# Equal pieces in the mixed expert units, shorter arithmetic of a recurrence, and filter spectra summed in PSUM: a hybrid backbone layer on one Trainium2 core

## Chip, core and metric

The kernel runs on one core of one Trainium2 chip. The metric is device microseconds of one execution, as the median over runs. The core's engines are TensorE (PE, with its weight loads PEld), VectorE (DVE), ScalarE (ACT), GpSimd (POOL) and SyncE (SP), which issues the DMA transfers here.

## What is computed

One layer (depth 1, batch 1) over 512 latent tokens of width 1024, with 256 context tokens ahead of them. All data are f32. Cut to what matters:

```python
p  = modulate(rmsnorm(x),   sh1, sc1)   @ w_in      # sh.., sc.., g.. from silu(c) @ w_ada + b_ada
pc = modulate(rmsnorm(ctx), csh1, csc1) @ w_in
# head group A: width 512, both directions, context first, then latents
u = dwconv(p[:, 512:1024])                          # 4 taps
r, i = sigmoid(block_diag(u, wa, ba)), sigmoid(block_diag(u, wx, bx))
log_a = -8 * r * softplus(-lam)
a, b = exp(log_a), sqrt(-expm1(2 * log_a)) * (i * u)
h[t] = a[t] * h[t-1] + b[t]                         # linear scan
ya = gelu(p[:, :512]) * (h_forward + h_backward)
# head group B: two long convolutions with generated filters
z = v
for o in range(2): z = gates[o] * (irfft(rfft(z, 1024) * rfft(g[o] / sum|g[o]|)) + z * fb[o])
x = x + g1 * (concat(rmsnorm(ya), rmsnorm(z)) @ w_out)
# MoE: best of 4 groups, best 2 of its 8 experts, 32 experts in all
h = modulate(rmsnorm(x), sh2, sc2)
for e: out += combine[:, e] * ((silu(h @ w_gate[e]) * (h @ w_up[e])) @ w_down[e])
return rmsnorm(x + g2 * out) * final_g
```

## The kernel before

Every operation is first recorded and then put in order by a list scheduler (class Recorder): it plays the engines forward with a cost for each operation, repeats this with changed priorities, and the best order found is emitted, with a sequence of its own for each engine. So all recorded work stands at two lines of the profile, L560 (a fixed engine) and L567 (operations written for `X`, where the scheduler may choose DVE, ACT or POOL). A change of one operation can move others.

*Filters* (`filters`, L980). For each of two orders `o`, `ab` holds two combinations (i = 0, 1) of the filter, each with its positions taken apart by residue r modulo 4. `dft` (L1023) multiplies the 128 positions of a residue by a table `dff[:, r, cs]` (cosine or sine) into a PSUM bank. The four outputs of an (o, i) are sums and differences of these transforms, the residues 0 and 2 in one, 1 and 3 in the other. Before the change each residue's product stands in a bank of its own; three of the six are copied to SBUF (`dft_s`), sums go to the tile `PM`, and sums of PM's parts are the outputs.

*Recurrence* (`lru_pair`, L1235, called twice, for two blocks of 128 channels each, the tokens of context and latents in 768 columns). `split` (L1182) takes an f32 operand apart into a rounded part (type fp32r, which PE passes once) and the rest, so that three rounded products stand for one f32 product. Here it was used for the gate weights `lw` and for `v`. The root is written as sqrt(tanh(-log_a) * (a*a + 1)), with DVE's product a*a ahead of the sum.

*Experts.* Each expert has a fixed number of token places (CAPS: sorted by load, the first three 64, then 192, 128, 128, 96, nine of 64, fifteen of 32, one of none). The token places are gathered in 14 units of 128 rows at most; a unit is a list of segments (first column, width, expert, first token) of width 64 or 32. Most units are uniform: two segments of 64 or four of 32. Two are mixed, 64 + 32 + 32: the last of kind M (the odd expert of 64 with two of 32) and the last of kind H (the expert of 96 with one of 32). ORDER, "MMHMQHQAMHQ", says in which order units follow the first three experts, so the mixed ones are the third last and the second last. `expert_units` (L1852) records a unit's work; its inner function `product` (L1870) accumulates gate (8 steps of 128 rows), up (8) and down (two halves of 4): in a step each segment has one matmul, whose token columns are the stationary tile at columns p0 to p0 + w of the array and whose 512 weight columns stream through. The segments' output goes to rows p0 to p0 + w of one PSUM bank.

The weights come in loads of 1 MB (`load`, L1801, issued at L1818), six for each expert, into a ring of 16 slots; a load waits until PE has used what its slot held. The loads stand on SP's queue in the order of use; those behind the first three experts also need the routing's result, since the expert's number is read from it.

The main lines of `product`:

```python
for i, (k, kk, h) in enumerate(parts):
    for (p0, w), wv in zip(sub[0], sub[2]):
        o = T.matmul(b[p0:p0 + w, :nc_], lhs[:, k, p0:p0 + w], wv(m, kk, h)[:, c0:c0 + nc_], start=i == 0,
                     stop=i == len(parts) - 1, tile_position=(0, p0), skip_group_check=True)
```

Of the kernel before, what the change touches and what calls it, by code (L numbers as in the profile page):

```python
# [742 lines left out]
def kernel(ctx: ExitStack, tc: tile.TileContext, a: dict, out: bass.AP, dbg=None):  # L743
# [35 lines left out]
    def give(*vs):  # L779
        for v in vs:  # L780
            v.home.give(v)
# [13 lines left out]
    class Fixed:  # L795
        n = 0
# [106 lines left out]
    SP.dma_start(out=dff[:], in_=a["c_dff"])  # L903

# [75 lines left out]
    def filters(o):  # L980
# [14 lines left out]
        for r in range(4):  # L995
            mab = take("mab", [512])
            mbb = take("mbb", [512])
            S.activation(mab[:], ab[:, 0, r], AF.Abs)
            S.activation(mbb[:], ab[:, 1, r], AF.Abs)
            X.tensor_tensor(mab[:], mab[:], mbb[:], op=OP.max)  # L1000
            give(mbb)
            T.matmul(b[32 * r:32 * r + 32, :], onesf, mab[:], start=True, stop=True,
                     tile_position=(0, 32 * r), skip_group_check=True)
            give(mab)
# [18 lines left out]
        def dft(i, cs, r):  # L1023
            b = ps()
            T.matmul(b, dff[:, r, cs], ab[:, i, r], start=True, stop=True)
            return b

        def dft_s(i, cs, r):
            b = dft(i, cs, r)
            t = take("fa", [512])  # L1030
            X.copy(t[:], b)
            return t

        for i in range(2):
            PM = take("PM", [4, 512])
            t = dft_s(i, i, 2)
            b = dft(i, i, 0)
            V.tensor_tensor(PM[:, 0], b, t[:], op=OP.add)
            V.tensor_tensor(PM[:, 2], b, t[:], op=OP.subtract)
            give(t)  # L1040
            t = dft_s(i, i, 3)
            b = dft(i, i, 1)
            V.tensor_tensor(PM[:, 1], b, t[:], op=OP.add)
            give(t)
            t = dft_s(i, 1 - i, 3)
            b = dft(i, 1 - i, 1)
            V.tensor_tensor(PM[:, 3], b, t[:], op=OP.subtract)
            give(t)
            for g, (p_, op) in enumerate(((0, OP.add), (0, OP.subtract), (2, (OP.add, OP.subtract)[i]),
                                          (2, (OP.subtract, OP.add)[i]))):  # L1050
                t = take("gout", [512])
                X.tensor_tensor(t[:], PM[:, p_], PM[:, p_ + 1], op=op)
                SP.dma_start(out=gd[o, i, g], in_=t[:])
                give(t)
            give(PM)
# [63 lines left out]
    give(*decs, hd, fbias)  # L1119
# [59 lines left out]
    V.tensor_scalar(ncoef, t8[4], 16.0, None, op0=OP.mult)  # L1179


    def split(src, wh, wl):  # L1182

        X.copy(wh, src)
        X.tensor_tensor(wl, src, wh.bitcast(F32), op=OP.subtract)
# [34 lines left out]
    lwH, lwL = (takeR("lw", [16, 128]) for _ in range(2))  # L1220
    split(lw, lwH, lwL)
    give(lw)
# [12 lines left out]
    def lru_pair(blks):  # L1235
        vs, sts = {}, {}
# [20 lines left out]
        for bk, v in vs.items():  # L1257
            st = sts[bk] = takeR("vst", [2048], late=True)
            X.copy(st[:, :768], v)
            X.tensor_tensor(st[:, 768:1536], v, st[:, :768].bitcast(F32), op=OP.subtract)  # L1260
        its = [(bk, d) for bk in blks for d in range(2)]
        rt, it = {}, {}
        for bk, d in its:
            for m, (dst, bn) in enumerate(((rt, "ba"), (it, "bx"))):
                g = take("g", [768])
                gi = (d * 2 + m) * 4 + bk
                b1, b2 = ps(), ps()
                for b, c0, n in ((b1, 0, 256), (b2, 256, 512)):
                    for j, (w, o) in enumerate(((lwH, 0), (lwH, 768), (lwL, 0))):
                        T.matmul(b[:, :n], w[:, gi], sts[bk][:, o + c0:o + c0 + n], start=j == 0, stop=j == 2)  # L1270
                S.activation(g[:, :256], b1[:, :256], AF.Sigmoid, bias=col(bn, 4 * d + bk))
                S.activation(g[:, 256:], b2, AF.Sigmoid, bias=col(bn, 4 * d + bk))
                dst[bk, d] = g
        give(*sts.values())
        at, bt = {}, {}
# [3 lines left out]
        for bk, d in its:  # L1279
            at[bk, d] = take("at", [768])  # L1280
            S.activation(at[bk, d][:], rt[bk, d][:], AF.Exp, scale=coef[:, 4 * d + bk:4 * d + bk + 1])
            S.activation(rt[bk, d][:], rt[bk, d][:], AF.Tanh, scale=ncoef[:, 4 * d + bk:4 * d + bk + 1])
            q = take("q", [768])
            X.tensor_tensor(q[:], at[bk, d][:], at[bk, d][:], op=OP.mult)
            V.scalar_tensor_tensor(rt[bk, d][:], q[:], 1.0, rt[bk, d][:], op0=OP.add, op1=OP.mult)
            give(q)
        for bk, d in its:
            S.activation(rt[bk, d][:], rt[bk, d][:], AF.Sqrt)
            X.tensor_tensor(rt[bk, d][:], rt[bk, d][:], it[bk, d][:], op=OP.mult)
# [188 lines left out]
    while left:  # L1478
        k = left.pop(0)
        i = int(k[1:] or 0)  # L1480
        if k[0] == "L":
            lru_pair((i, i + 1))
            if not [x for x in left if x[0] == "L"]:
                give(lwH, lwL)
# [367 lines left out]
    def expert_units(subs, need=lambda m: None, then=lambda: None, last=False):  # L1852
# [17 lines left out]
        def product(sub, m, lhs, parts, c0=0, nc_=512):  # L1870
            b, before = ps(), None
            for i, (k, kk, h) in enumerate(parts):
                for (p0, w), wv in zip(sub[0], sub[2]):
# [163 lines left out]
```

## Time and profile before

| | us |
|---|---|
| median of 3 runs | 927.65 |
| lowest and highest | 925.95, 929.68 |
| the profiled execution | 931.36 |
| its span in the profile | 929.6 |
| granted TensorE clock, mean | 0.971 of full speed |

How to read it: the span runs from the first to the last instruction of the profiled execution. PE, PEld, DVE, ACT and POOL are busy times of engines, which overlap. In the tables by stage the numbers behind an x count instructions; PEclk is the granted TensorE clock as a part of full speed, DMA the mean busy share of the 16 DMA engines. Names such as bank (a PSUM bank), slot and arena (pieces of SBUF that the kernel hands out) are the program's. An f32 matmul leaves two records in PE's rows, a rounded one (fp32r) one.

### The profile page before, as it was taken

How to read it: one execution, taken by the hardware profiler on the slowest of the kernel's cores; microseconds unless marked ns; L12 is line 12 of the kernel's file. 1: busy time of each engine (PE TensorE's matmuls, PEld its weight loads, DVE VectorE, ACT ScalarE, POOL GpSimd, SP SyncE). 2: the span in 40 equal slices, each digit the busy share in tenths (PEclk: the TensorE clock that was granted, in tenths of full speed). 3: DMA queues.
4: the chain of work that ended last, by engine and by line, in shares of the span. 5: the costliest groups of instructions: out<-in, count | busy, mean ns of one | idle time of the engine just before them, and what ended most of it. 6: DMA issues, size and time to landing. Idle time of an engine off the chain costs nothing.

```text
span 929.6 us, 13429 instructions
## 1 busy us (share of the span) xinstructions
PE 855.6 (92%) x5282; PEld 453.6 (49%) x5283; DVE 507.3 (55%) x971; ACT 279.9 (30%) x511; POOL 23.6 (3%) x25
## 2 busy tenths in 40 slices
PE   3988998899999799599999999999999999999984
PEld 0344674578887577435544444453554323233332
DVE  7989889599999977604233322431413214212135
ACT  4678188764345124301211110120110100000014
POOL 0000001010003000000000000000000000000002
PEclk9989999799999899799999999999999999999997
DMA  9985377333423596398999989999999999876693
GB/s 292 414 276 195 103 238 218 135 118 120 148 80 131 187 327 223 119 361 306 367 386 386 386 294 359 388 386 386 386 387 386 386 387 382 321 281 223 231 335 142
DMA packets 132618, 259.73 MB, mean 279 GB/s; under 512 B 6928, under 2 KB 28432, under 8 KB 129606
## 3 DMA queue, kind: packets, MB, share of 16 engines
q1 hardware_dynamic: 132534, 258.81, 77.7%
q8 instruction: 43, 0.70, 0.3%
q14 instruction: 25, 0.20, 0.1%
q10 hardware_dynamic: 16, 0.02, 0.0%
HBM read 252.49 MB, written 6.31 MB: 278 GB/s over the span
## 4 chain that ended last, share of the span: by engine, by line
PE 68%; DVE 7%; DMA 1%; ACT 1%; issue 0%; SPq 0%; DVEq 0%; ACTq 0%
PE bank L560 68%; DVE arena L567 2%; DVE slot L567 2%; DVE arena L560 2%; DMA slot<-in_w_down_dram 1%; DVE slot L560 1%; ACT slot L560 0%; DVE R L560 0%; DVE rsb_in L560 0%; DVE fine L560 0%; ACT arena L560 0%; ACT slot L567 0%; SPq L1818 0%; DVE finy L560 0%; DVE hy L560 0%
## 5 line engine op out<-in xcount | busy, mean ns | idle before, releaser
L560 PE MATMUL bank<-arena 128*64 128x512 f32 (+8 forms) x1434 | 314.6, 533 | 26.0 <-DMA arena<-in_b_ada_dram 5.9
L560 PE MATMUL bank<-slot 128*128 128x512 f32 (+1 forms) x1064 | 282.8, 410 | 14.9 <-DVE slot L567 4.8
L560 PE MATMUL bank<-slot,arena 128*64 128x512 f32 (+2 forms) x936 | 242.9, 597 | 1.9 <-DMA slot<-in_w_down_dram 0.9
L560 PEld LDWEIGHTS bank<-slot 128*128 128x128 f32 x1064 | 195.2, 193 | 99.5 <-issue 27.3
L560 PEld LDWEIGHTS bank<-arena 128*32 128x32 f32 (+5 forms) x1434 | 100.5, 132 | 166.8 <-issue 117.5
L560 DVE TENSOR_TENSOR arena<-arena,bank 128x512 f32<-128x512 f32 (+2 forms) x131 | 80.5, 663 | 167.4 <-PE bank L560 167.2
L567 DVE TENSOR_TENSOR arena<-arena 128x512 f32<-128x512 f32 (+3 forms) x142 | 120.6, 886 | 2.5 <-DMA arena<-in_w_dram 1.8
L560 PEld LDWEIGHTS bank<-slot,arena 128*64 128x64 f32 (+1 forms) x936 | 58.3, 124 | 111.6 <-issue 101.0
L560 ACT ACTIVATE arena<-bank 128x512 f32<-128x512 f32 (+1 forms) x66 | 38.3, 595 | 243.4 <-PE bank L560 240.8
L560 PEld LDWEIGHTS <-slot 128*128 128x128 bf16 x1344 | 76.9, 98 | 40.9 <-issue 40.6
L560 PE MATMUL bank<-R,slot 128*128 128x128 bf16 x1344 | 88.7, 220 | 0.3 <-ACT arena L567 0.3
L567 DVE TENSOR_SCALAR arena<-bank,A2c,B2c 128x128 f32<-128x128 f32 x36 | 14.6, 410 | 115.6 <-PE bank L560 115.5
L567 ACT ACTIVATE arena<-bank,B2c,A2c 128x128 f32<-128x128 f32 x76 | 30.7, 454 | 137.1 <-DVE arena L567 85.4
L560 ACT ACTIVATE slot<-arena 128x512 fp32r<-128x512 f32 (+2 forms) x43 | 27.7, 645 | 113.5 <-DVE arena L560 104.2
L560 DVE SCALAR_TENSOR_TENSOR arena<-bank,iw,arena 128x512 f32<-128x512 f32 (+1 forms) x29 | 21.2, 732 | 69.6 <-PE bank L560 69.2
L560 PE MATMUL bank<-ident,arena 128*128 128x128 f32 (+2 forms) x234 | 40.7, 292 | 5.2 <-ACT arena L567 2.2
L560 ACT ACTIVATE arena<-arena 128x512 f32<-128x512 f32 (+6 forms) x59 | 32.7, 589 | 26.5 <-DVE arena L560 21.4
L560 PEld LDWEIGHTS bank<-ident,arena 128*128 128x128 f32 (+2 forms) x234 | 30.2, 160 | 19.9 <-issue 5.7
L567 ACT ACTIVATE slot<-slot 128x1024 fp32r<-128x1024 f32 (+1 forms) x32 | 26.4, 846 | 28.4 <-DVE slot L567 22.9
L567 DVE TENSOR_TENSOR slot<-slot 128x1024 fp32r<-128x1024 f32 (+1 forms) x35 | 33.7, 974 | 0.1
L560 ACT ACT_TABLE_LOAD x23 | 29.5, 1283 | 6.0 <-DMA arena<-in_pack_dram 4.6
L560 DVE TENSOR_TENSOR arena<-bank,arena 128x512 f32<-128x512 f32 (+1 forms) x42 | 27.7, 680 | 5.5 <-PE bank L560 3.1
(172 smaller groups left out, 417.3 us busy)
## 6 DMA issues: line engine op xcount, KB each, us to landing
arena<-in_w_down_dram SPq DMA_DIRECT2D x41, 1024.0 KB, 13.5
slot<-in_w_up_dram SPq DMA_DIRECT2D x39, 1024.0 KB, 14.0
slot<-in_w_gate_dram SPq DMA_DIRECT2D x32, 1024.0 KB, 13.6
arena<-in_w_gate_dram SPq DMA_DIRECT2D x30, 1024.0 KB, 11.8
arena<-in_w_up_dram SPq DMA_DIRECT2D x23, 1024.0 KB, 9.4
slot<-in_w_down_dram SPq DMA_DIRECT2D x20, 1024.0 KB, 10.3
arena<-in_w_ada_dram SPq DMA_DIRECT2D x32, 512.0 KB, 5.1
slot<-in_w_ada_dram SPq DMA_DIRECT2D x8, 1024.0 KB, 11.1
```

The costliest lines, as they stand in the source:

```text
L560: return self.rec.add(self.name, lambda: f(*[real(v) for v in args], **{k: real(v) for k, v in kw.items()}), outs, ins, cost, **x)
L567: return cost, lambda: f(*[real(v) for v in args], **{k: real(v) for k, v in kw.items()}), port
```

## The change

Three things are changed.

1. In `product` every segment is cut into pieces of the unit's narrowest width. In a mixed unit the segment of 64 becomes two pieces of 32 that stream the same weights; uniform units stay as they are.
2. In the recurrence neither `lw` nor `v` is split: the gate products are one f32 product each, and `lw` stays where it was loaded until the second call has ended. The root is written as (a + 1) * sqrt(tanh(-log_a / 2)), so the product a*a goes, and the multiply-add stands behind ACT's root rather than ahead of it.
3. In the filters two residues are added up in one bank (a table `dfn` with the sign changed, made once on ACT, serves for the differences): eight matmuls for each (o, i), two copies to SBUF, four sums that read PSUM directly; `PM` goes. One maximum is written for DVE, no longer for a free choice.

```diff
@@ -901,6 +901,8 @@
     negt = part("negt")
     dff = take("dff", [4, 2, 128], top=True)
     SP.dma_start(out=dff[:], in_=a["c_dff"])
+    dfn = take("dfn", [2, 2, 128])
+    S.activation(dfn, dff[:, 2:], AF.Copy, scale=-1.0)
 
     w3s = [[take("w3", [2, 512]) for _ in range(2)] for _ in range(2)]
     for o in range(2):
@@ -997,7 +999,7 @@
             mbb = take("mbb", [512])
             S.activation(mab[:], ab[:, 0, r], AF.Abs)
             S.activation(mbb[:], ab[:, 1, r], AF.Abs)
-            X.tensor_tensor(mab[:], mab[:], mbb[:], op=OP.max)
+            V.tensor_tensor(mab, mab, mbb, op=OP.max)
             give(mbb)
             T.matmul(b[32 * r:32 * r + 32, :], onesf, mab[:], start=True, stop=True,
                      tile_position=(0, 32 * r), skip_group_check=True)
@@ -1020,39 +1022,31 @@
         V.tensor_tensor(ab[0:1, 0, 0], ab[0:1, 0, 0], fl[0:1, :], op=OP.add)
         give(l4)
 
-        def dft(i, cs, r):
+        def dft(i, *terms):
             b = ps()
-            T.matmul(b, dff[:, r, cs], ab[:, i, r], start=True, stop=True)
+            for j, (d_, cs, r) in enumerate(terms):
+                T.matmul(b, d_[:, r % d_.shape[1], cs], ab[:, i, r], start=not j, stop=j == len(terms) - 1)
             return b
 
-        def dft_s(i, cs, r):
-            b = dft(i, cs, r)
+        def dft_s(i, *terms):
             t = take("fa", [512])
-            X.copy(t[:], b)
+            X.copy(t, dft(i, *terms))
             return t
 
         for i in range(2):
-            PM = take("PM", [4, 512])
-            t = dft_s(i, i, 2)
-            b = dft(i, i, 0)
-            V.tensor_tensor(PM[:, 0], b, t[:], op=OP.add)
-            V.tensor_tensor(PM[:, 2], b, t[:], op=OP.subtract)
-            give(t)
-            t = dft_s(i, i, 3)
-            b = dft(i, i, 1)
-            V.tensor_tensor(PM[:, 1], b, t[:], op=OP.add)
-            give(t)
-            t = dft_s(i, 1 - i, 3)
-            b = dft(i, 1 - i, 1)
-            V.tensor_tensor(PM[:, 3], b, t[:], op=OP.subtract)
-            give(t)
-            for g, (p_, op) in enumerate(((0, OP.add), (0, OP.subtract), (2, (OP.add, OP.subtract)[i]),
-                                          (2, (OP.subtract, OP.add)[i]))):
+
+            odd = dft_s(i, (dff, i, 1), (dff, i, 3))
+            b = dft(i, (dff, i, 0), (dff, i, 2))
+            gs = [(b, OP.add, odd), (b, OP.subtract, odd)]
+            odd = dft_s(i, (dff, 1 - i, 1), (dfn, 1 - i, 3))
+            b = dft(i, (dff, i, 0), (dfn, i, 2))
+            gs += [(b, (OP.add, OP.subtract)[i], odd), (b, (OP.subtract, OP.add)[i], odd)]
+            for g, (b, op, odd) in enumerate(gs):
                 t = take("gout", [512])
-                X.tensor_tensor(t[:], PM[:, p_], PM[:, p_ + 1], op=op)
+                V.tensor_tensor(t, b, odd, op=op)
                 SP.dma_start(out=gd[o, i, g], in_=t[:])
                 give(t)
-            give(PM)
+            give(gs[0][2], odd)
         give(ab)
 
         V.tensor_tensor(cb[:, :, 4 * o:4 * o + 4], cb[:, :, 4 * o:4 * o + 4],
@@ -1116,7 +1110,7 @@
     xhs, tmps, nh = [take("xh", [D]) for _ in range(2)], [take("htmp", [4, 128]) for _ in range(NTMP)], [0, 0]
     for o in range(2):
         filters(o)
-    give(*decs, hd, fbias)
+    give(*decs, hd, fbias, dfn)
     give(modr[0], modT[0])
     hH, hL = ([takeR("h", [4, 512]) for _ in range(2)] for _ in range(2))
     cH, cL = ([takeR("c", [8, 256])] for _ in range(2))
@@ -1176,7 +1170,7 @@
     V.tensor_scalar(t8[0], t8[0], 0.0, 0.5, op0=OP.max, op1=OP.mult)
     V.tensor_tensor(t8[4], t8[4], t8[0], op=OP.add)
     V.tensor_scalar(coef, t8[4], -16.0, None, op0=OP.mult)
-    V.tensor_scalar(ncoef, t8[4], 16.0, None, op0=OP.mult)
+    V.tensor_scalar(ncoef, t8[4], 8.0, None, op0=OP.mult)
 
 
     def split(src, wh, wl):
@@ -1217,9 +1211,6 @@
         for h in range(2):
             split(st[:, 2 * h:2 * h + 2], *(w[:, 2 * h:2 * h + 2] for w in UW[i]))
         give(st)
-    lwH, lwL = (takeR("lw", [16, 128]) for _ in range(2))
-    split(lw, lwH, lwL)
-    give(lw)
     ct = [take("ct", [512]) for _ in range(2)]
     for j in range(2):
         b = ps()
@@ -1233,7 +1224,7 @@
     give(*cH, *cL)
 
     def lru_pair(blks):
-        vs, sts = {}, {}
+        vs = {}
         for bk in blks:
             bc = ps()
             for j in range(2):
@@ -1254,10 +1245,6 @@
             vs[bk] = v
         if blks[-1] == 3:
             give(*UW[0], *UW[1], *ct)
-        for bk, v in vs.items():
-            st = sts[bk] = takeR("vst", [2048], late=True)
-            X.copy(st[:, :768], v)
-            X.tensor_tensor(st[:, 768:1536], v, st[:, :768].bitcast(F32), op=OP.subtract)
         its = [(bk, d) for bk in blks for d in range(2)]
         rt, it = {}, {}
         for bk, d in its:
@@ -1266,13 +1253,11 @@
                 gi = (d * 2 + m) * 4 + bk
                 b1, b2 = ps(), ps()
                 for b, c0, n in ((b1, 0, 256), (b2, 256, 512)):
-                    for j, (w, o) in enumerate(((lwH, 0), (lwH, 768), (lwL, 0))):
-                        T.matmul(b[:, :n], w[:, gi], sts[bk][:, o + c0:o + c0 + n], start=j == 0, stop=j == 2)
+                    T.matmul(b[:, :n], lw[:, gi], vs[bk][:, c0:c0 + n], start=True, stop=True)
                 S.activation(g[:, :256], b1[:, :256], AF.Sigmoid, bias=col(bn, 4 * d + bk))
                 S.activation(g[:, 256:], b2, AF.Sigmoid, bias=col(bn, 4 * d + bk))
                 dst[bk, d] = g
-        give(*sts.values())
-        at, bt = {}, {}
+        at = {}
         for bk, d in its:
             X.tensor_tensor(it[bk, d][:], it[bk, d][:], vs[bk][:], op=OP.mult)
         give(*vs.values())
@@ -1280,12 +1265,10 @@
             at[bk, d] = take("at", [768])
             S.activation(at[bk, d][:], rt[bk, d][:], AF.Exp, scale=coef[:, 4 * d + bk:4 * d + bk + 1])
             S.activation(rt[bk, d][:], rt[bk, d][:], AF.Tanh, scale=ncoef[:, 4 * d + bk:4 * d + bk + 1])
-            q = take("q", [768])
-            X.tensor_tensor(q[:], at[bk, d][:], at[bk, d][:], op=OP.mult)
-            V.scalar_tensor_tensor(rt[bk, d][:], q[:], 1.0, rt[bk, d][:], op0=OP.add, op1=OP.mult)
-            give(q)
         for bk, d in its:
+
             S.activation(rt[bk, d][:], rt[bk, d][:], AF.Sqrt)
+            V.scalar_tensor_tensor(rt[bk, d][:], at[bk, d][:], 1.0, rt[bk, d][:], op0=OP.add, op1=OP.mult)
             X.tensor_tensor(rt[bk, d][:], rt[bk, d][:], it[bk, d][:], op=OP.mult)
         for bk in blks:
             hf, hb = it[bk, 0], it[bk, 1]
@@ -1481,7 +1464,7 @@
         if k[0] == "L":
             lru_pair((i, i + 1))
             if not [x for x in left if x[0] == "L"]:
-                give(lwH, lwL)
+                give(lw)
         elif k[0] == "M":
             (mod_second, mod_third)[i - 1]()
         elif k[0] in "vab":
@@ -1869,8 +1852,11 @@
 
         def product(sub, m, lhs, parts, c0=0, nc_=512):
             b, before = ps(), None
+
+            one = min(w for _, w in sub[0])
+            turns = [(p, one, wv) for (p0, w), wv in zip(sub[0], sub[2]) for p in range(p0, p0 + w, one)]
             for i, (k, kk, h) in enumerate(parts):
-                for (p0, w), wv in zip(sub[0], sub[2]):
+                for p0, w, wv in turns:
                     o = T.matmul(b[p0:p0 + w, :nc_], lhs[:, k, p0:p0 + w], wv(m, kk, h)[:, c0:c0 + nc_], start=i == 0,
                                  stop=i == len(parts) - 1, tile_position=(0, p0), skip_group_check=True)
                     if not REC.direct:
```

Three places of the engines' orders. First PE, at the start of the first mixed unit's products (bank_70 and bank_69 take its gate and up sums; a row's shape is that of the output, "x2" two of the same kind behind each other). Before:

```order
L560 MATMUL bank_70<-slot,arena 64x512
L560 MATMUL bank_70<-arena 32x512 x2
L560 MATMUL bank_70<-slot,arena 64x512
L560 MATMUL bank_70<-arena 32x512 x2
L560 MATMUL bank_70<-slot,arena 64x512
L560 MATMUL bank_70<-arena 32x512 x2
L560 MATMUL bank_70<-slot,arena 64x512
L560 MATMUL bank_70<-arena 32x512 x2
L560 MATMUL bank_70<-arena 64x512
L560 MATMUL bank_70<-slot,arena 32x512 x2
```

With the change:

```order
L560 MATMUL bank_69<-slot,arena 64x512 x8
L560 MATMUL bank_70<-arena 32x512 x18
L560 MATMUL bank_70<-slot,arena 32x512 x2
L560 MATMUL bank_70<-arena 32x512 x2
L560 MATMUL bank_70<-slot,arena 32x512 x2
L560 MATMUL bank_70<-arena 32x512 x2
L560 MATMUL bank_70<-slot,arena 32x512 x2
L560 MATMUL bank_70<-arena 32x512 x2
L560 MATMUL bank_70<-slot,arena 32x512 x2
L560 MATMUL bank_72<-slot 128x512
```

Where a piece of 64 and two of 32 took turns, all pieces are now of 32, and one kind stands next to itself; what is ahead of this place has the same order in both.

Second PE, in the transforms of the filters (arena to a bank, 128x512). Before:

```order
L560 MATMUL bank_74<-arena 128x512
L560 MATMUL bank_67<-arena,sel_87 32x512
L560 MATMUL bank_69<-arena 128x512
L560 MATMUL bank_70<-arena 128x512
L560 MATMUL bank_71<-arena 128x512
L560 MATMUL bank_72<-arena 128x512
L560 MATMUL bank_68<-slot,arena 32x512 x4
L560 MATMUL bank_73<-ident,arena 128x32 x4
L560 MATMUL bank_74<-arena 128x512
L560 MATMUL bank_67<-arena 128x512
```

With the change:

```order
L560 MATMUL bank_69<-arena 128x512
L560 MATMUL bank_70<-arena 128x512
L560 MATMUL bank_71<-ident,arena 128x128 x4
L560 MATMUL bank_70<-arena 128x512
L560 MATMUL bank_74<-arena 128x512
L560 MATMUL bank_69<-arena 128x512
L560 MATMUL bank_72<-arena 128x512 x2
L560 MATMUL bank_73<-arena 32x512 x4
L560 MATMUL bank_73<-arena 32x256 x4
L560 MATMUL bank_67<-arena 128x512 x2
L560 MATMUL bank_68<-ident,arena 128x32 x4
```

Before, each transform had a bank to itself; now some stand in pairs in one bank, with other work (32-row products, transposes) between them.

Third DVE, in the first pair of blocks of the recurrence (768 columns; slot is the rounded operand). Before:

```order
L567 CAST slot<-arena 128x768
L560 TENSOR_TENSOR cb<-cb,inv 128x3x4
L567 TENSOR_TENSOR slot<-arena,slot 128x768
L560 TENSOR_TENSOR arena<-bank_73,arena 128x512
L567 TENSOR_TENSOR arena<-arena 128x512
L567 COPY arena<-bank_67 128x512
L567 TENSOR_TENSOR arena<-arena 128x512
L567 TENSOR_TENSOR arena<-arena 128x768
L560 SCALAR_TENSOR_TENSOR arena<-arena 128x768
```

With the change:

```order
L560 TENSOR_TENSOR arena<-arena,B2c 128x512
L560 TENSOR_REDUCE wrB<-arena 128x64
L560 TENSOR_TENSOR arena<-bank_72,arena 128x512 x2
L567 TENSOR_TENSOR arena<-arena 128x768 x3
L560 SCALAR_TENSOR_TENSOR arena<-arena 128x768
L567 TENSOR_TENSOR arena<-arena 128x768
L560 SCALAR_TENSOR_TENSOR arena<-arena 128x256
L560 SCALAR_TENSOR_TENSOR arena<-arena 128x512
```

The copies and differences into slot are gone, and products of 768 columns stand ahead of the multiply-add without a product a*a.

## Rows read from the trace of the kernel before

**Rows 1.** The page's busy time, share of the span and instructions of each engine.

```profile
PE 855.6 (92%) x5282; PEld 453.6 (49%) x5283; DVE 507.3 (55%) x971; ACT 279.9 (30%) x511; POOL 23.6 (3%) x25
```

**Rows 2.** Busy time by stage: stretch, length, PE, PEld, DVE, ACT, POOL, PEclk, DMA, GB/s.

```profile
0.00:206.80 206.80, 173.51 (x928) 103.78 (x929) 180.39 (x350) 136.72 (x222) 6.43 (x11) 0.96 0.65 222
383.10:600.00 216.90, 216.87 (x1574) 103.64 (x1574) 68.57 (x149) 33.42 (x68) 0.97 (x4) 0.99 0.94 342
600.00:757.50 157.50, 156.44 (x1221) 70.21 (x1219) 45.79 (x97) 20.47 (x42) 0.00 (x0) 1.00 1.05 386
757.50:896.00 138.50, 138.20 (x703) 43.29 (x706) 35.60 (x60) 11.30 (x22) 0.00 (x0) 1.00 0.83 298
896.00:930.00 34.00, 17.90 (x144) 8.52 (x136) 14.15 (x49) 12.12 (x36) 4.97 (x4) 0.84 0.57 203
```

**Rows 3.** The chain of waits: start, us, engine and work.

```profile
383.13 232.22 PE bank L560 x1760
...
776.25 119.12 PE bank L560 x630
...
896.49 10.68 DMA slot<-in_w_down_dram
...
907.21 6.96 PE bank L560 x63
```

**Rows 4.** SP's waits from 380 to 930 us: total, times, longest.

```profile
SPq L1818 <- PE bank L560: 301.8, 105, 13.0
```

**Rows 5.** PE's timeline, uniform units, then a mixed one: start, us, work.

```profile
442.62 7.09 PE L560 MATMUL bank<-arena 128*64 128x512 f32 x32
...
600.56 3.64 PE L560 MATMUL bank<-arena 128*32 128x512 f32 x32
...
757.51 1.05 PE L560 MATMUL bank<-arena 128*32 128x512 f32 x4
758.49 1.07 PE L560 MATMUL bank<-slot,arena 128*64 128x512 f32 x2
759.49 1.05 PE L560 MATMUL bank<-arena 128*32 128x512 f32 x4
```

**Rows 6.** Busy time in two stretches about the last weights' landing.

```profile
907.00:910.00 3.00, 2.79 (x17) 1.30 (x17) 1.27 (x3) 0.55 (x2) 0.00 (x0) 1.00 0.84 295
910.00:912.00 2.00, 2.00 (x34) 1.05 (x33) 1.41 (x4) 2.00 (x8) 0.39 (x1) 1.00 0.03 12
```

**Rows 7.** Busy time in a stretch in which PE waits.

```profile
374.00:378.00 4.00, 0.00 (x0) 0.00 (x0) 4.00 (x11) 1.48 (x3) 0.00 (x0) 0.50 0.54 208
```

**Rows 8.** DVE's groups by form, 0 to 206 us: count, busy, mean ns, idle before.

```profile
L567 DVE TENSOR_TENSOR arena<-arena 128x768 f32<-128x768 f32 x24 | 21.9, 950 | 0.3 <-ACT arena L560 0.2
...
L567 DVE TENSOR_TENSOR arena<-arena 128x512 f32<-128x512 f32 x31 | 20.8, 684 | 2.1 <-DMA arena<-in_w_dram 1.8
L567 DVE TENSOR_TENSOR slot<-arena,slot 128x512 fp32r<-128x512 f32 x12 | 11.6, 963 | 0.1
...
L567 DVE TENSOR_TENSOR slot<-arena,slot 128x768 fp32r<-128x768 f32 x4 | 3.8, 950 | 0.0
...
L567 DVE CAST slot<-arena 128x512 fp32r<-128x512 f32 x5 | 2.9, 579 | 0.0
...
L567 DVE TENSOR_TENSOR slot<-arena,slot 128x2048 fp32r<-128x2048 f32 x1 | 2.3, 2284 | 0.0
...
L567 DVE CAST slot<-arena 128x768 fp32r<-128x768 f32 x3 | 1.7, 560 | 0.0
...
L567 DVE CAST slot<-arena 128x2048 fp32r<-128x2048 f32 x1 | 1.2, 1226 | 2.0 <-DMA arena<-in_lw_dram 2.0
```

**Rows 9.** PE's timeline at two places, and one of its groups by form.

```profile
38.50 3.70 PE L560 MATMUL bank<-arena 128*128 128x512 f32 x8
...
129.17 8.06 PE L560 MATMUL bank<-slot 128*128 128x512 f32 x37
...
L560 PE MATMUL bank<-arena 12*32 12x512 f32 x24 | 4.5, 836 | 6.6 <-DMA arena<-in_b_ada_dram 5.9 <-DVE he L560 0.7
```

## Prediction

> **What bounds the kernel now.** I read the page's busy lines first. TensorE (PE) is busy in 92% of the span and VectorE (DVE) in 55% [rows 1]. A share over the whole span says little here, because the program has stages with different limits, so next I read the busy time by stage [rows 2]. In the first 206.8 us, where the filters and the recurrence lie, PE is busy 173.5 us and DVE 180.4: two engines that are both nearly full, and neither leads clearly. From 383.1 on the experts run. To 600 PE is busy all the time at 342 GB/s; to 757.5 PE is still full, but the DMA share is 1.05 at 386 GB/s, so both limits meet; from 757.5 to 896 PE is busy for 138.2 of 138.5 us while the rate falls to 298 GB/s. So in that last stretch PE alone sets the pace and the weights wait for it.
>
> The chain of waits says the same from the other side: two pieces of PE work of 232.2 and 119.1 us carry it from 383 to 896, and only then comes a step that waits for a weight load [rows 3]. SP's waits give the reason why the loads slow down: 301.8 us of waiting, in 105 places, at the line that issues weight loads, each for a ring slot that PE has not yet released [rows 4]. The timeline of PE shows what it does so long [rows 5]. In a uniform unit 32 records take 7.09 us with two pieces of 64 columns (8 steps of the sum, 0.89 us each) and 3.64 us with four pieces of 32 (4 steps, 0.91 us each): all pieces of a step run beside each other. In a unit of 64, 32 and 32 columns one step goes from 757.51 to 759.49, that is 1.98 us, and in it the piece of 64 and the pair of 32 stand behind each other, about 1 us each. (An f32 matmul leaves two records.)
>
> **The change part by part.** *Equal pieces.* Two units are mixed, each with 24 steps (8 for gate, 8 for up, 2 x 4 for down), so 48 steps go from 1.98 us to 0.90, the mean of the two uniform rows: 48 x 1.08 = 52 us of PE work. The number of matmul instructions in such a step rises from three to four, all of equal width. The order of PE's instructions before these units stays as it was, and so does the order of the loads. But the 52 us are not all to be had, since the weights are the next limit. From 757.5 to 896 come 298 x 138.5 = 41.3 MB. After 896 come 203 x 34 = 6.9 MB [rows 2], less the output (512 x 1024 x 4 bytes = 2.1 MB) and an estimated 0.5 MB of a last vector spread over the partitions: 4.3. These 45.6 MB at 386 GB/s take 118 us, while PE's own work there would shrink to 138.2 - 52 = 86. The last weights then land at 757.5 + 118 = 876 us. Now they land near 910: the rate is 295 GB/s in the 3 us before and 12 in the 2 us behind [rows 6]. **Gain 34 us.** What lies behind the last landing (19.6 us to the end of the span) stays.
>
> The halves of a mixed step last 0.98 to 1.00 us where a whole uniform step lasts 0.90 [rows 5]. The Trainium skill, "TensorEngine Tiling (Array Packing)", section "Key Properties", says that another tiling mode, not just another tile, drains the engine. By the drain alone each half would cost the extra 0.09 us, and to remove it would give 48 x 2 x 0.09 = 9 us; by the rows the halves also take turns, and that gives 52. No stretch of the trace shows the drain by itself. I take the rows' 52, because uniform units of either width show the same step time.
>
> *PE that now waits for weights.* With 86 us of work in 118, PE has gaps that it hasn't now. Where PE was idle (374 to 378 us) the granted clock was 0.50, the lower of the two levels, 1.2 GHz [rows 7]; where it works without a gap it is 1.00 [rows 2]. Only work behind the last weights can lengthen the end. If the last 6.96 us of the chain [rows 3] ran at the lower level they would take 7 us more; if the bursts keep the clock up, nothing. I take +3, since the stretch behind 896, which already waits for weights, has a mean clock of 0.84 and not 0.5 [rows 2].
>
> *Recurrence, DVE.* By the order of instructions in both kernels up to the end of the recurrence (the cover of the filters included), these go from DVE: nine sums of 768 (8.6 us), four of 768 into a rounded operand (3.8), one of 2048 (2.3), the three casts of 768 and the one of 2048 (2.9), thirteen sums of 512 (8.9). These come: six copies of 512 (3.5) and three sums of 512 into rounded operands (2.9), which other engines do now. Sum -20 us [rows 8]. The multiply-add of the new formula (a+1 times the root) takes the place of one that stood ahead of the root; its price stays, but it now waits for ACT. Behind it on DVE stands the product with i*v and then the scan. Cost: nothing, since four chains of it run beside each other.
>
> *PE in the same part.* Eight transforms of the filters more: eight records of such an f32 matmul take 3.70 us, so four matmuls, 0.93 us each [rows 9], +7.4. A gate product had three rounded passes on 512 and on 256 columns. 37 rounded ones of 512 take 8.06 us, 0.22 each [rows 9]; by columns the three passes cost 0.65 + 0.33 = 0.98, and the f32 products now 0.93 + 0.46 = 1.39. Sixteen gates: +6.6. PE therefore gains 14 us of work, and has 206.8 - 173.5 = 33 idle there [rows 2]. The four sums per filter that read PSUM directly, and the loss of one copy out of three, are in DVE's sum above. A spectrum's bank is now held for two sums; PE has six others.
>
> What -20 on DVE and +14 on PE give together, no row shows. If DVE decides alone, -20; if PE does, the added work may lengthen the stretch: I bound that by +5, a third of the 14 us, since PE's idle time would hold all of it twice but needn't lie where the work lies. I take the middle, **-8**, and keep both ends.
>
> **Sum:** -34 + 3 - 8 = -39. The profiled run took 931.4 us (its span 929.6), 3.7 above the median of 927.65; counted from the median the forecast is **888 us**.
>
> **The rivals.**
> 1. *PE takes over in the first part.* It is 84% busy there against DVE's 87%, and both become PE's 90% and DVE's 78%. Then the gain of 8 is none or a loss of 5: 896 to 901. For it: the gates' products now come in one piece ahead of ACT's sigmoids. Against: DVE loses more work than PE gets. 0.20.
> 2. *DVE's gain comes whole.* -20 in place of -8: 876. For it: PE's 33 idle us hold the added 14 twice. Against: a part of that idle time is PE waiting for results of ACT and for loads, which the change doesn't make earlier. 0.13.
> 3. *PE's clock falls between bursts of weights.* For it: the gaps of 32 us in all. If a third of the 86 us ran at the lower level, some 29 us of PE time would come on top, which the 32 us of gaps take up but for the tail; with the tail's 7 and a late slot or two of 2 to 3 us it is 894 to 898. Of such a loss the Trainium skill, "TensorE: Matmul & The Clock Gate", section "HAM oscillation — how this bites in real kernels", tells in a matmul kernel whose bursts are shorter than its waits for DMA; the 0.50 of [rows 7] agrees that idle time costs clock. 0.10.
> 4. *Two pieces that stream the same expert's rows go in turns of two.* Then a step takes 2 x 0.90 = 1.80 us, the gain is 48 x 0.18 = 9, too little for the weights to matter: 927.65 - 9 - 8 = 911. 0.04.
> 5. *Slower: the four pieces of a step run one behind another,* because pairs of them read one weight tile. The place is the same 48 steps; each would take 4 x 0.90 = 3.60, or 78 us more, less 8: 998. It decides for slower as soon as a step takes more than 1.98 + 8/48 = 2.15 us. Against it: 24 small matmuls over twelve rows, all with the same vector streamed, take 4.5 us of busy time at 836 ns each [rows 9], a sum of 20 us if they stood one behind another; and four pieces of different experts already run together [rows 5]. 0.02.
> 6. The change doesn't do what it says in the mixed units (another order keeps them apart): -8 alone, 920. The order printed for both kernels speaks against it. 0.01.
>
> **How the numbers follow.** My forecast has the remaining 0.50, with a range of its own from 881 to 893. The first three rivals reach from 876 to 901; with a few us for the bounds on either side the range is 869 to 904, and outside it lie rivals 4 to 6 and the ends of the others, some 0.15 to 0.2. About 0.5% (4.6 us) is what a measurement can tell from no change: faster than 923 are all cases but the fifth, and a little of the sixth and of unknown faults: 0.95 faster, 0.02 the same, 0.03 slower.
>
> **What would show it.** In the changed profile the steps of the mixed units should be 0.9 us long, four pieces of 32 side by side; the DMA rate should be near 386 GB/s until the last weights; SP's wait at the load line should shrink well below 301.8 us; PE should show idle time released by the weights' DMA, some 30 us behind 740; and the first stage should end 8 us earlier (between 20 earlier and 5 later). Wrong would be: a mixed step of 1.8 us or more, a rate under 350 GB/s behind the mixed units' start, or a start of the experts that is later than before.

## The result and the profile after

The changed kernel takes 894.88 us (median of 4 runs, 893.52 to 896.14) against 928.52 us of the kernel before (4 runs): a ratio of 0.964, 95% interval 0.961 to 0.967, so 33.6 us less. Forecast was 888, with a range from 869 to 904. The profiled execution took 896.14 us, its span 894.2.

Busy time by stage of the changed kernel, cut at the same places of the program (columns as in [rows 2]), and four short stretches about the end:

```profile
0.00:206.80 206.80, 188.70 (x944) 107.31 (x946) 170.13 (x334) 132.96 (x215) 8.25 (x11) 1.00 0.68 236
...
379.80:597.00 217.20, 217.19 (x1573) 104.02 (x1572) 68.52 (x148) 33.42 (x68) 0.97 (x4) 0.99 0.94 341
597.00:740.00 143.00, 142.05 (x1166) 66.40 (x1165) 42.64 (x89) 18.32 (x38) 0.00 (x0) 1.00 1.05 386
740.00:828.00 88.00, 86.13 (x726) 36.97 (x724) 30.95 (x57) 12.29 (x24) 0.00 (x0) 1.00 1.05 386
828.00:862.00 34.00, 27.56 (x157) 8.05 (x149) 7.70 (x12) 1.23 (x2) 0.00 (x0) 0.90 1.05 387
862.00:872.00 10.00, 6.41 (x43) 2.08 (x44) 1.44 (x2) 1.23 (x2) 0.00 (x0) 1.00 1.05 381
...
872.00:874.00 2.00, 2.00 (x10) 1.06 (x8) 1.17 (x2) 0.44 (x1) 0.00 (x0) 1.00 0.72 243
874.00:876.00 2.00, 2.00 (x30) 1.06 (x29) 1.39 (x3) 2.00 (x8) 0.00 (x0) 1.00 0.39 143
876.00:878.00 2.00, 2.00 (x32) 1.22 (x27) 0.48 (x1) 1.63 (x4) 0.46 (x1) 1.00 0.04 16
```

The rate no longer falls to 298 GB/s where the mixed units begin: it stays at 381 to 387 up to 872 us, and the last weights land at 876. From 740 to 872 PE has 11.9 idle us (1.87, 6.44 and 3.59 in the three rows), where it had 0.3 in the stretch from 757.5 to 896 before. PE's timeline in the first mixed unit shows what has become of the 1.98 us of [rows 5]:

```profile
757.80 0.60 PE L560 MATMUL bank<-arena 128*32 128x512 f32 x2
757.82 0.60 PE L560 MATMUL bank<-slot,arena 128*32 128x512 f32 x2
758.23 0.60 PE L560 MATMUL bank<-arena 128*32 128x512 f32 x2
758.25 0.60 PE L560 MATMUL bank<-slot,arena 128*32 128x512 f32 x2
758.66 0.60 PE L560 MATMUL bank<-arena 128*32 128x512 f32 x2
758.68 0.60 PE L560 MATMUL bank<-slot,arena 128*32 128x512 f32 x2
```

Each pair of lines is one half of a step (four pieces, each with the first or the second of its two records) and the next begins 0.43 us later, so a step takes 0.86 us. The chain of waits now has loads in it well ahead of the end, and SP's waits (same view as [rows 4], from 380 us; the line that issues the loads is now L1801) are shorter:

```profile
379.81 233.00 PE bank L560 x1759
...
828.91 14.38 DMA slot<-in_w_up_dram
...
856.37 13.98 DMA arena<-in_w_down_dram
...
870.40 8.48 PE bank L560 x70
```

```profile
SPq L1801 <- PE bank L560: 248.3, 111, 13.8
```

Cut at the start of the experts (383.1 before, 379.8 now) and at the last landing (910 and 876), the 35.4 us between the two spans are 3.3 of the first part, 30.7 of the experts up to the landing, and 1.4 behind it. So the experts' part is near the forecast's term, and the first part is less than half of it. Was that the arithmetic, or something else?

### The profile page after: what moved, and what is told of

Same layout as the page of the kernel before. It is cut to its first block, busy times and chain, and to the rows that moved or that the text cites. A ratio compares the mean times of both kernels' runs of the same rounds, so it can differ in the third digit from the quotient of the medians.

```text
span 894.2 us, 13529 instructions
## 1 busy us (share of the span) xinstructions
PE 820.8 (92%) x5362; PEld 445.8 (50%) x5363; DVE 488.2 (55%) x947; ACT 274.8 (31%) x500; POOL 17.6 (2%) x21
## 4 chain that ended last, share of the span: by engine, by line
PE 78%; DVE 11%; DMA 6%; SPq 2%; issue 1%; ACT 1%; DVEq 0%; ACTq 0%
PE bank L560 78%; DVE arena L567 5%; DVE slot L567 3%; DVE arena L560 2%; DMA slot<-in_w_up_dram 2%; DMA arena<-in_w_down_dram 2%; DMA slot<-in_w_ada_dram 1%; SPq L1801 1%; DMA arena<-in_w_dram 1%; DVE slot L560 1%; DMA arena<-in_x_dram 1%; ACT arena L560 0%; SPq L560 0%; ACT slot L560 0%; ACT arena L567 0%
## 5 line engine op out<-in xcount | busy, mean ns | idle before, releaser
L560 PE MATMUL bank<-arena 128*32 128x512 f32 (+7 forms) x1546 | 315.6, 532 | 35.6 <-DVE arena L567 10.4
L560 PE MATMUL bank<-slot 128*128 128x512 f32 x968 | 266.6, 415 | 8.2 <-ACT slot L560 3.2
L560 PEld LDWEIGHTS bank<-slot 128*128 128x128 f32 x968 | 176.6, 189 | 89.2 <-issue 33.2
L560 PE MATMUL bank<-slot,arena 128*32 128x512 f32 (+2 forms) x1000 | 209.1, 598 | 2.3 <-DMA slot<-in_w_ada_dram 1.3
L560 PEld LDWEIGHTS bank<-arena 128*32 128x32 f32 (+4 forms) x1546 | 110.7, 134 | 173.6 <-issue 126.1
L567 DVE TENSOR_TENSOR arena<-arena 128x512 f32<-128x512 f32 (+3 forms) x111 | 99.7, 937 | 12.8 <-ACT arena L560 8.8
L560 PEld LDWEIGHTS bank<-slot,arena 128*32 128x32 f32 (+1 forms) x1000 | 54.7, 123 | 92.4 <-issue 79.0
L567 ACT ACTIVATE arena<-bank,B2c,A2c 128x128 f32<-128x128 f32 x76 | 30.7, 455 | 150.7 <-DVE arena L567 81.4
L567 ACT ACTIVATE slot<-slot 128x1024 fp32r<-128x1024 f32 (+1 forms) x34 | 28.3, 857 | 54.5 <-DVE slot L567 37.0
L560 ACT ACTIVATE arena<-arena 128x512 f32<-128x512 f32 (+6 forms) x60 | 33.6, 590 | 29.4 <-DVE arena L560 19.4
## 6 DMA issues: line engine op xcount, KB each, us to landing
slot<-in_w_up_dram SPq DMA_DIRECT2D x38, 1024.0 KB, 14.2
```

Of the source, the lines that this page charges most:

```text
L560: return self.rec.add(self.name, lambda: f(*[real(v) for v in args], **{k: real(v) for k, v in kw.items()}), outs, ins, cost, **x)
L567: return cost, lambda: f(*[real(v) for v in args], **{k: real(v) for k, v in kw.items()}), port
```

## The experiments

All runs are compared with the kernel before on the same chip. "Start" is the start of the experts in the profiled execution, read to about 0.1 us, "from there" the rest of its span. In the kernel before these are 383.1 and 546.5 us, in the changed one 379.8 and 514.4.

**The parts alone.** First the equal pieces by themselves, in the kernel before:

```diff
+            one = min(w for _, w in sub[0])
+            turns = [(p, one, wv) for (p0, w), wv in zip(sub[0], sub[2]) for p in range(p0, p0 + w, one)]
             for i, (k, kk, h) in enumerate(parts):
-                for (p0, w), wv in zip(sub[0], sub[2]):
+                for p0, w, wv in turns:
```

> The kernel before with equal pieces alone; filters and recurrence as before. Theory A (the equal pieces carry the change, the weights' rate bounds them): 31 to 35 us less than before, some 894 to 897 us, with the DMA rate at 386 GB/s to the last weights and PE waiting for weights behind 740 us. Rival B (the forecast's other term is real too: the first part of the kernel gives 8 us and the pieces only some 26): 901 us or more.

Measured: 891.07 us, ratio 0.957 (0.954 to 0.960), 38.6 us less than before: more than the whole change gives. Start 375.1, from there 515.3. The second number is theory A's: 31 us less than before. The first is the surprise: the start is 8.0 us earlier, though not one operation ahead of the experts was changed.

Then the recurrence alone (the change's lines in `lru_pair`, and no `lwH`, `lwL`):

```diff
-                    for j, (w, o) in enumerate(((lwH, 0), (lwH, 768), (lwL, 0))):
-                        T.matmul(b[:, :n], w[:, gi], sts[bk][:, o + c0:o + c0 + n], start=j == 0, stop=j == 2)
+                    T.matmul(b[:, :n], lw[:, gi], vs[bk][:, c0:c0 + n], start=True, stop=True)
```

> The kernel before with the recurrence's shorter arithmetic alone. By the forecast's rows PE gets 6.6 us more and DVE loses some 17. Theory A (PE sets the pace of the part ahead of 261 us): between 2 us less and 6 us more than before. Rival C (DVE sets it): 8 to 17 us less.

Measured: 918.37 us, ratio 0.987 (0.985 to 0.990), 11.3 us less; start 371.9, from there 544.6. Taken alone it speaks for rival C.

The filters alone (the change's lines in `filters`):

```diff
-            PM = take("PM", [4, 512])
+            odd = dft_s(i, (dff, i, 1), (dff, i, 3))
+            b = dft(i, (dff, i, 0), (dff, i, 2))
```

> The kernel before with the filters' sums in PSUM alone. PE gets 7.4 us more, DVE loses a few sums. Theory A (PE sets the pace): the same to 7 us more than before. Rival C (DVE sets it): 2 to 8 us less.

Measured: 927.21 us, ratio 0.998 (0.995 to 1.001): nothing that can be told. Start 378.8, from there 546.8.

Both of them, without the equal pieces:

```diff
-                for p0, w, wv in turns:
+                for (p0, w), wv in zip(sub[0], sub[2]):
```

> The changed kernel without the equal pieces: recurrence and filters together. Theory A: 1 to 4 us less than before (the experts start 3.3 us earlier in the changed kernel's trace). Rival B: 8 us less. Rival D (the order that the list scheduler happens on decides over a few us, not the work): it differs from the sum of the two parts measured alone by more than 3 us.

Measured: 922.38 us, ratio 0.992 (0.990 to 0.995), 7.2 us less; start 374.9, from there 544.7. Near rival B's 8 us, but it differs from the two parts' sum (13.7) by 6.4, as rival D has it. And the parts don't add up to the whole: 38.6 + 7.2 is 45.8, where the change gives 33.6. What adds up is the part from the start on: 546.5, 544.6, 546.8 and 544.7 without equal pieces, 514.4 and 515.3 with them, 31 us. What doesn't is the start. In this kernel and the changed one the work ahead of the experts is the same, and the starts differ by 4.9 us; the two with the old arithmetic differ by 8.0.

**Order or work.** So the next runs hold the work fixed and change the order, or the other way round. First the gate products again in three rounded passes, with all else as changed:

```diff
-                    T.matmul(b[:, :n], lw[:, gi], vs[bk][:, c0:c0 + n], start=True, stop=True)
+                    for j, (w, o) in enumerate(((lwH, 0), (lwH, 768), (lwL, 0))):
+                        T.matmul(b[:, :n], w[:, gi], sts[bk][:, o + c0:o + c0 + n], start=j == 0, stop=j == 2)
```

> The changed kernel with the gate products in three rounded passes again (lw and v split as before); root, filters and equal pieces as changed. PE gets some 6.6 us less than in the changed kernel, DVE some 9 more. Theory A (PE sets the pace ahead of the experts): their start comes 4 to 7 us earlier than in the changed kernel (379.8 us in its trace). Rival C (DVE does): 5 to 9 us later. Theory D (the order that the scheduler draws weighs more than a few us of work): no rule, anything from 370 to 384 us.

Measured: 891.20 us, ratio 0.958 (0.956 to 0.959); start 374.6, from there 516.0. 5.2 us earlier than the changed kernel, which is theory A's number, but also inside what an order alone does, so it doesn't decide.

> Recurrence and equal pieces, the filters as before. If the part ahead of the experts and the experts' part add up (start of the experts 371.9 us as with the recurrence alone, and 514 to 516 us from there, as in both kernels with equal pieces): a span of 886 to 888, some 888 to 890 us, less than either kernel. If an earlier start only makes PE wait longer for weights: 892 or more.

The edit is the recurrence's and the product's, as above. Measured: 888.93 us, ratio 0.956 (0.954 to 0.958); start 372.4, from there 514.5. The two parts add up. The list scheduler put the first part in the same order here as with the recurrence alone, row for row, and the start came out at 372.4 and 371.9.

Then the same work in other orders, by the time within which the scheduler lets an urgent operation go ahead:

```diff
-LOOK = 50
+LOOK = 40
```

> The changed kernel, the same work, with another order: LOOK, the time in ns within which the list scheduler takes a later but more urgent operation, is 40 in place of 50. Theory D: the experts start 4 us or more away from 379.8. Theories A and C (the work of the fullest engine sets it): within 2 us of it.

Measured: 886.77 us, ratio 0.953 (0.951 to 0.955); start 369.7, from there 516.0.

> The kernel before with equal pieces (filters and recurrence as before) and LOOK 40: the same work as with equal pieces alone, whose experts start at 375.1, where the same work started at 383.1 in the kernel before. Theory D: a third value, 3 us or more away from 375.1. Theories A and C: within 2 us of 375.1 (or of 383.1).

Measured: 884.44 us, ratio 0.950 (0.949 to 0.952); start 367.4, from there 515.9. A third value, 7.7 us from 375.1.

```diff
-LOOK = 50
+LOOK = 60
```

> The changed kernel with LOOK 60: the same work in a third order. Theory D (the order decides the first part, the work of recurrence and filters nothing that shows): the experts start somewhere from 367 to 381 us, and within 6 us of the next run's start, of either sign; from there 514 to 516 us to the end. Theory A or C (the parts' work counts): the difference to the next run has the sign and the size of the pairs measured so far only by chance.

Measured: 887.24 us, ratio 0.955 (0.953 to 0.956); start 368.1, from there 514.7.

> Equal pieces alone (recurrence and filters as before) with LOOK 60, beside the run ahead of it. Theory D: experts' start from 367 to 381 us. Were the shorter recurrence and the filters worth the 8 us of the forecast, this one would start 8 us later than the changed kernel with the same LOOK.

Measured: 894.21 us, ratio 0.961 (0.959 to 0.963); start 377.9, from there 514.9. It starts 9.8 us later than the changed kernel with the same LOOK. The expectation's 6 us were too narrow, and this pair alone would bear out the forecast's 8. But the other two pairs with equal pieces are 4.7 and 2.3 us the other way. The first part of six kernels with equal pieces, each up to its start (busy times as in [rows 2]); the old arithmetic at LOOK 50, 40 and 60:

```profile
0.00:375.10 375.10, 321.12 (x1650) 226.14 (x1652) 344.05 (x626) 196.92 (x332) 16.90 (x18) 0.95 0.60 204
```

```profile
0.00:367.40 367.40, 319.98 (x1650) 225.85 (x1652) 339.35 (x621) 200.95 (x342) 7.66 (x12) 0.96 0.60 209
```

```profile
0.00:377.90 377.90, 320.48 (x1650) 224.59 (x1652) 340.93 (x606) 198.22 (x341) 43.66 (x27) 0.96 0.58 202
```

and the changed arithmetic, also at LOOK 50, 40 and 60:

```profile
0.00:379.80 379.80, 331.62 (x1634) 222.00 (x1636) 324.91 (x594) 197.43 (x332) 11.65 (x13) 0.97 0.58 202
```

```profile
0.00:369.70 369.70, 327.42 (x1634) 221.18 (x1636) 328.82 (x594) 197.44 (x326) 21.82 (x19) 0.98 0.60 207
```

```profile
0.00:368.10 368.10, 326.74 (x1634) 223.30 (x1636) 325.89 (x592) 199.88 (x332) 19.27 (x19) 0.97 0.60 208
```

The work shows in every row: DVE is busy 339 to 344 us with the old arithmetic and 325 to 329 with the new, PE 320 to 321 and 327 to 332. The start doesn't follow it: a mean of 373.5 for the old and 372.5 for the new, while either work by itself spreads over 10 to 12 us with its order. The medians say the same: 891.07, 884.44 and 894.21, mean 889.9; 894.88, 886.77 and 887.24, mean 889.6. These three pairs don't settle what the new arithmetic is worth. The fourth pair, without equal pieces (the kernel before and the one with both other parts), has it 8.2 us ahead in the start (383.1 and 374.9) and 7.2 in the median. Over all four it is ahead by 2.8 us in the start and 2.0 in the median, with single pairs from 4.7 behind to 9.8 ahead in the start: too few draws to tell a few us from nothing.

**What is left of the experts' part.** With LOOK 40 and equal pieces alone, the order of the units:

```diff
-ORDER = "MMHMQHQAMHQ"
+ORDER = "QHMMMMHQAHQ"
```

> Equal pieces alone with LOOK 40 (experts start at 367.4, 515.9 us from there) and another order of units: ORDER QHMMMMHQAHQ, one unit of four experts of 32 first and then one of a single expert of 128. If what is left of the experts' part is the loads that stand still behind their start because PE has not released slots, while PE waits for weights at the end: 5 to 20 us less than with the old order, 865 to 880 us, PE's waits behind 740 us smaller. If PE's own work is the limit now too: within 4 us of 884.4.

Measured: 878.05 us, ratio 0.945 (0.943 to 0.946), 6.4 us under the same kernel with the old order, and the fastest of all; start 363.4, from there 510.6, which is 5.3 less. Its two stretches of the experts, and those of the kernel with the old order under them:

```profile
363.40:600.00 236.60, 236.32 (x1709) 112.06 (x1709) 71.73 (x154) 34.85 (x71) 0.98 (x4) 0.99 0.97 355
600.00:850.00 250.00, 246.96 (x1942) 107.70 (x1940) 83.74 (x165) 27.72 (x53) 0.00 (x0) 1.00 1.04 382
```

```profile
367.40:600.00 232.60, 232.50 (x1759) 112.67 (x1760) 73.72 (x162) 35.37 (x73) 0.97 (x4) 0.99 0.94 343
600.00:860.00 260.00, 248.01 (x1896) 105.34 (x1890) 78.19 (x148) 30.97 (x61) 0.00 (x0) 0.99 1.05 386
```

The loads run at 355 in place of 343 GB/s up to 600 us, and PE's idle time behind it falls from 12.0 to 3.0 us. That is near the lower end of what was expected: with 3.0 us of idle time left behind 600, PE's own work is now the limit there. The order of the first part is the same in both, row for row on PE, DVE and ACT, and yet the starts are 4.0 us apart. The two ran on different chips, where the kernel before took 929.89 and 929.87 us, and the orders of the loads differ behind the first experts; which of this moved the start is open. So the start in one profile is good to about 4 us, not better.

> The same with ORDER MQMMHMHQHAQ: a unit of four experts of 32 second, the unit pair of the expert of 192 next to last. The same two cases: 865 to 880 us, or within 4 us of 884.4.

Measured: 880.85 us, ratio 0.948 (0.946 to 0.950); start 365.2 (the order of the first part is again the same), from there 512.2, which is 3.7 less: the same effect, a little smaller.

## Why the prediction was right, and what of it was not

**The equal pieces: right.** The step came out at 0.86 us, where 0.90 was taken from [rows 5]. That the 52 us of PE work would not all come, because the weights are the next limit at 386 GB/s, is what the stages show. Forecast was a gain of 34 us, measured are 30.7 up to the landing in this pair; from the start to the end of the span the four kernels without equal pieces take 545.7 us on average and the eight with them, in the old order of units, 515.2, so 30.5. The last weights were forecast at 876 us and landed at 876, but the start 3.3 us earlier is in that, so that they agree to the microsecond is partly luck. The estimate of bytes was a little low (386 GB/s from 754.6 to 872 are 45.3 MB, and some 0.8 came behind at 243 and 143 GB/s), and those last 4 us did not run at the full rate.

**PE's gaps: right in kind, 32 us forecast and 11.9 measured.** The 86 us held only the work that stood ahead of 896, while the 118 us reach to what then stood at 910: some 10.7 us of PE work more by the same view of the kernel before. The rest is work that did not go away: from the start to the end of the span PE's busy time fell from 529.4 to 489.2 us, 40.2 in place of the 52 forecast, and from 754.6 to 872 PE is busy 105.5 us. So the 0.86 us hold for steps that run unbroken, not for all 48. Part of why shows in rows like this one (start, us, work, the wait ahead of it):

```profile
848.72 1.05 PE L560 MATMUL bank<-arena 128*32 128x512 f32 x2 [1.67 <-DMA arena<-in_w_up_dram]
```

A piece that waited for its weights runs alone, and its two records take 1.05 us, more than a whole step of four. How much of the 12 us this makes up was not measured.

**The clock's +3: not there.** Where PE waits for weights, from 828 to 862, the granted clock is 0.90 in the mean. That is one fall towards the lower level, 1.2 GHz (0.60 from 852 to 856 and 0.54 to 860), after a stretch from 848 to 852 in which PE was busy for 1.62 of 4 us. Behind the last weights, from 874 to 878, it is 1.00, and the stretch behind the landing (18.2 us) is no longer than before (19.6). The rule in the Trainium skill, "TensorE: Matmul & The Clock Gate", section "HAM oscillation — how this bites in real kernels", agrees with the trace that far: bursts between waits for DMA do lower the clock. Here the lowered clock lay beside the loads, and cost nothing that shows at the end. The 9 us that the rule of the page "TensorEngine Tiling (Array Packing)" of the Trainium skill, section "Key Properties", would give by the drain alone, an estimate, are less than a third of the 30.7 measured; how much of a mixed step was drain, no run tells apart.

**The first part's -8: this is the term that failed.** It was mis-sized: 3.3 us in this pair, and its ground is not borne out. In the first 206.8 us PE got 15.2 us more work (14 forecast) and DVE 10.3 less (20 forecast); up to the start DVE went from 343.2 to 324.9 us and PE from 326.2 to 331.6. But the start does not follow them, as the six rows show.

The term took PE's 33 idle us as room for the added work, with the warning that they needn't lie where the work lies. Most of them did not. The first two rows are of the kernel before, the next two of the changed one (columns as in [rows 2]), and the last is from the changed kernel's chain of waits (start, us, work):

```profile
0.00:100.00 100.00, 73.86 (x364) 34.39 (x366) 90.10 (x233) 64.23 (x125) 0.79 (x8) 0.97 0.79 280
100.00:206.00 106.00, 98.85 (x563) 68.83 (x562) 89.49 (x116) 72.50 (x98) 5.64 (x3) 0.95 0.52 168
...
0.00:100.00 100.00, 81.94 (x424) 35.07 (x426) 85.10 (x229) 58.43 (x115) 0.79 (x8) 1.00 0.92 324
100.00:206.00 106.00, 105.96 (x518) 71.60 (x517) 84.23 (x105) 74.44 (x101) 7.46 (x3) 1.00 0.46 152
...
100.63 111.51 PE bank L560 x543
```

Before, 26.1 of the idle us lay ahead of 100 us and 7.2 behind. In the changed kernel 18.1 of those ahead are still idle, but PE is busy all the time from 100 to 206, and the chain runs through PE alone from 100.6 to 212.1: in this stretch PE took over, as rival 1 has it. That alone does not set the start either: with LOOK 40 and 60 PE is busy for 104.65 and 106.00 of the same 106 us, and the experts start some 10 us earlier.

The prediction's sentence that the multiply-add's new wait for ACT costs nothing, "since four chains of it run beside each other", was wrong about DVE. These are two of DVE's groups of 768 columns in the changed kernel, the sums and the multiply-add, from 0 to 206 us, to be held against [rows 8]:

```profile
L567 DVE TENSOR_TENSOR arena<-arena 128x768 f32<-128x768 f32 x15 | 13.9, 950 | 7.0 <-ACT arena L560 6.9
...
L560 DVE SCALAR_TENSOR_TENSOR arena<-arena 128x768 f32<-128x768 f32 x8 | 7.5, 955 | 7.3 <-ACT arena L560 7.3
```

The sums of 768 columns went from 24 to 15 as forecast, and 14.2 us of waiting for ACT stand ahead of these two groups, where 0.2 stood ahead of the first one before. The waits ahead of the sums vary with the order in either arithmetic. But in the same view of the changed arithmetic at LOOK 40 and 60 the multiply-add waits 5.8 and 3.4 us, with the old one 0.1 or less at every LOOK. So some of the 18 us that DVE saves is spent waiting: in the two groups together 14.2 us of waits against 3.1 with the old arithmetic at LOOK 50, but only some 4 us more than there at LOOK 40 and 60. Nor do these waits set the start: the recurrence alone has 17.4 us of them, more than the changed kernel, and starts at 371.9.

Why so little is left of the first part in this pair thus stays open. PE's full stretch and DVE's waits are both there, and neither orders the starts. Shown is that the order of the list scheduler moves the start by 10 to 16 us with the work unchanged, more than the whole term, and that four pairs, with a mean of 2.0 us in the median, can tell the new arithmetic's worth neither from nothing nor from the forecast's 8. By its time alone rival 3 (894 to 898) fits as well as any, but the clock behind the landing speaks against it; rival 1 (no gain in the first part, 896 to 901) came nearest by what happened in the trace, though its range missed by 1 us and its cause is not shown to set the start.

**The range and the middle.** The range held because the experts' term carried it. Between the two profiled spans the sum of -39 came out at -35.4: the first part gave 4.7 us less than forecast and the experts 3.3 less, and the tail 4.4 more (3 of the clock, and 1.4). The other 3 us to 895 lie mostly in the step from the profiled run to the median: it stood 3.7 us above the median that was known before, and 1.3 above it now. Another 0.65 is rounding: 927.65 less 39 is 888.65, which the prediction gave as 888.

## What to carry to other kernels

When a scheduler writes the order, a change of one part draws a new order for all others: compare kernels by stage, and draw several orders for the same work before a few us are put down to the work; here three or four pairs were not enough for that. Pieces of equal width on the array's columns ran side by side here (0.86 to 0.91 us a step), and a step of 64, 32 and 32 columns paid for each width in turn (1.98 us). What a stage gives back is bounded by the next limit in line, and that bound (bytes left, divided by the rate seen where the transfers run unbroken) can be had from the trace before anything is built.

## What the runs showed that was not expected

Four 32-column pieces of which two stream the same weights end in 0.86 us an unbroken step, no more than four of different experts (0.91). The order alone, with the same operations, moved the start of the experts from 383.1 to 375.1 and 367.4 us, almost half of the gain of the whole change, though a start in one profile is good to about 4 us only. And the unit order that takes a unit of four experts first is worth 5.3 us more from the start on, where PE had looked full up to 600 us and the loads behind it.
